# Differential attention on 128 rows for both score passes, and post-norm weights kept with the row buffers

## The chip, the cores and the metric

The kernel runs on one core of one Trainium2 chip. The core has engines that each work through a list of their own in order and wait for each other by semaphores: TensorE (PE) for matrix products, VectorE (DVE), ScalarE (ACT) and GpSimd (POOL) for work on rows and tiles, and SyncE (SP), which issues the transfers between the chip's memory and the core's buffers. PE reads its operands from SBUF and adds up in banks of PSUM; the other engines read PSUM and free the banks. The metric is the time of one execution in microseconds (us), as the device measures it; of several runs the median counts. Three runs of the kernel before took 2561.74, 2572.24 and 2570.22 us, median 2570.22 us.

## What is computed

A decoder trunk of two layers on 1024 tokens of width 1024, in float32. Each layer is a SwiGLU network (FFN), a token mixer and another FFN, each between two norms. The first layer's mixer is a hybrid: 4 heads of differential attention and 4 of gated linear attention (GLA) behind one projection; the second's is stick-breaking attention with 8 heads. The part that the change touches:

```python
def diff_attention(q, k, v, lam_params, subln_g, lambda_init):
    lp = lam_params.astype(f32)
    lam = jnp.exp(jnp.sum(lp[0] * lp[1])) - jnp.exp(jnp.sum(lp[2] * lp[3])) + lambda_init
    qf = q.astype(f32) * (DIFF_DH ** -0.5)          # 4 heads x 2 components, 64 wide each
    for i in range(s // Q_BLOCK):                   # 8 query tiles of 128
        sc = jnp.einsum('bqhd,bkhd->bhqk', qf[:, start:end], kf[:, :end])
        p = jax.nn.softmax(jnp.where(mask, sc, -jnp.inf), axis=-1)
        p = p[:, :, 0] - lam * p[:, :, 1]           # component 0 less lam times component 1
        outs.append(jnp.einsum('bhqk,bkhv->bqhv', p, vf[:, :end]))
    o = rmsnorm(jnp.concatenate(outs, axis=1), subln_g) * (1.0 - lambda_init)
```

Each sublayer ends in `h + rmsnorm(y, g)`, and the weights g of this norm (1024 numbers, read to all 128 partitions) are the tile `pg`.

## The kernel before

Activations and weights are split into a high and a low part, each as `fp32r`, and a product is taken as high x high, high x low and low x high: three matmuls (`mm3`, L210 to L212). A matmul contracts over the partitions (rows) of its operands, up to 128.

The scores of differential attention contract over 64 numbers only, so there the parts are stacked. For component c, `q_stack` puts the high parts of q in the 64 rows of that component and the low parts in the other 64 rows: `A[c]`. `k_stack` puts the high parts of k in both halves of `B[c]` (L687 on ACT, L705 on ACT), and the low parts in the component's own rows of a third tile, `L` (DVE, L688). `diff_attn` then gives `scores` two passes, `(q[c], k[c])` over 128 rows, which is high x high plus low x high, and `(q[c][r], k[2][r])` over the 64 rows r, which is high x low (both L763). For query tile i, `scores` makes one chunk of up to 512 keys (i = 0 to 3) or two chunks (i = 4 to 7), none narrower than 256 columns; the last chunk of a tile gets the causal mask added by a third, small matmul (L766). Per component and head that makes 4 x 1 + 4 x 2 = 12 chunks, so 4 x 2 x 12 = 96 chunks and 192 score matmuls. Stick-breaking uses the same `scores` with three passes that all have 128 rows.

A query tile goes on as follows. DVE takes the maxima (L874, L875), ACT the exponentials with their sums (L878), DVE the factors (L884 to L891) and `e0 - g e1` (L894); PE transposes it, four blocks to a group (`tps`, L778); DVE and ACT copy the groups to attention tiles (`att`, L780, pool `at_d` with 4 buffers); PE multiplies with v (`po`, L899); then ACT squares (L902), DVE takes the mean (L170), POOL the root (L172), DVE scales (`on`, L904), PE transposes (`pot`, L906) and ACT writes the output tile (L907). Between these steps stand the projections of the next head (`pps`, `vps`, L210 to L212), which `filled` hands out over the query tiles; in the last head it is the first part of the mixer's output projection (`dps`). The tiles of k of a head (three) are in pool `kk_d` with 6 buffers, so two heads' tiles are there at a time.

`pg` is loaded by `load_pg` (L471) to pool `ep`, which is open for the whole program. An FFN loads it before its first weights; a mixer at the head of its output projection in the program, and the scheduler moves the load up far ahead. An FFN's products with `pg` are L582, those of a mixer L419 (`fo`). The row buffers that the norms use (pools `fp` and `hrow`) are opened by `open_fo`. An FFN's down projection (`down_strassen`) loads its weights by `rawd` (L527, L535), while POOL still makes sums for the end of the up projection (L343 to L346).

At the start, `consts` builds masks: two causal ones (`mk_incl`, `mk_strict`), level masks for GLA (`lmf` on POOL, L126 to L131, cast by DVE to `lm`, L134) and loads the lambda parameters (`lp`, L138), from which ACT takes an exponential (`lexp`).

The framework's scheduler fixes each engine's list from the program's order and the buffers; the text of the program alone doesn't show it. SP's list is one queue: a load that waits holds up all behind it.

Of the kernel before, what the change touches and what calls it, by code (L numbers as in the profile page):

```python
# [9 lines left out]
F32 = mybir.dt.float32  # L10
# [9 lines left out]
P = 128  # L20
# [15 lines left out]
class Trunk:  # L36
# [25 lines left out]
    def open_fo(self):  # L62
        """row buffers of the norms"""
        self.foctx = ExitStack()
        self.fp = self.dyn(self.foctx, "fp", 4, side="right")
        self.hctx = ExitStack()
        self.hrow = self.dyn(self.hctx, "hrow", HB, side="right")

    def open_mix(self, cx, z, t, po):
        """PSUM banks of the mixers; the accumulators of the rest (self.mctx) may outlive the others"""  # L70
# [33 lines left out]
    def mixer_consts(self):  # L104
# [7 lines left out]
        # additive masks, rows q, columns k: NEG where k > q (incl) or k >= q (strict)  # L112
        self.mask = {}
        for nm, base in (("incl", 0), ("strict", -1)):
            m = c.tile([P, P], F32, name="mk_" + nm)
# [6 lines left out]
        # level masks: source row s in the even half of the block of target column t  # L122
        self.lmask = {}
        for lv in LEVELS:
            m = c.tile([P, 64], F32, name="lmf%d" % lv, tag="lmf")
# [10 lines left out]
        # lambda of the differential attention, on every partition  # L136
        lp = c.tile([P, 4, 64], F32, name="lp")
# [19 lines left out]
        # twice: the gate's first factor arrives in two parts, 16 rows each  # L157
# [85 lines left out]
    def make_raw(self, xns, gname, gi, pool):  # L243
        """gained, transposed k tiles, not split"""
# [28 lines left out]
    def gu(self, cx, wg, wu, A, xn1, gname, gi):  # L273
        """A: split k tiles of the first token half; xn1: rows of the second half.
        Returns per column tile, per token half [P, TB] = silu(gate) * up."""
# [23 lines left out]
        def combos(j):  # L299
            # S1 = A21 + A22, S3 = A11 - A21, S2 = S1 - A11, S4 = A12 - S2 (S3, then S4 in A21's place)  # L300
# [36 lines left out]
        for c in range(NF):  # L337
# [4 lines left out]
            # T1 = B12 - B11, T2 = B22 - T1, T3 = B22 - B12, T4 = B21 - T2  # L342
# [32 lines left out]
    def down_step(self, w, f0, H, f, KT, accs):  # L375
        """first column half, one K tile, all token tiles"""
# [7 lines left out]
    def down(self, w, H, pg, order=None, prep=None, mid=None, begun=None):  # L384
        """begun: accumulators of the first column half that hold all but the last K tile"""
# [45 lines left out]
    def epilogue(self, tb, fo, ss, half, hsrc, hdst, last):  # L431
        """fo: rows [P, D], or pairs of halves"""
# [36 lines left out]
    def load_pg(self, row):  # L469
        pg = self.ep.tile([P, D], F32, name="pg", tag="pg")  # L470
        self.nc.sync.dma_start(out=pg, in_=row.rearrange("(o d) -> o d", o=1).to_broadcast([P, D]))  # L471
        return pg
# [13 lines left out]
    def ffn(self, l, f, x0, xn1, hsrc, hdst, last):  # L486
# [5 lines left out]
        pg = self.load_pg(a["ffn_post_g"][l, f])  # L492
        ph = self.gu(cx, wg, wu, x0, xn1, "ffn_pre_g", 2 * l + f)
        self.open_fo()
        nxt = ("mix_pre_g", l) if f == 0 else ("ffn_pre_g", 2 * (l + 1))
# [5 lines left out]
    # ---- down projection of both token halves: one level of Strassen-Winograd over  # L501
    # (token half, half of the first 2 * KH k tiles, column half); the last k tile is added as it is ----
    def down_sums(self, ph, j):
        """S1 = A21 + A22, S3 = A11 - A21 (in A21's place) of k tile j"""
# [7 lines left out]
    def down_strassen(self, w, ph, pg, hsrc, hdst, nxt):  # L512
# [10 lines left out]
        def raw(j, k=None, cols=None):  # L523
            """[P, 2, TB]: both column halves of k tile j, or a column half of the two k tiles j, k"""
# [13 lines left out]
        # B11 = (j, 0), B12 = (j, 1), B21 = (j + KH, 0), B22 = (j + KH, 1)  # L538
# [51 lines left out]
        # P1 = A11 B11, P2 = A12 B21: C11 = P1 + P2  # L590
# [675 lines left out]
```

## Time and profile before

| | |
|---|---|
| median of 3 runs | 2570.22 us |
| lowest and highest run | 2561.74, 2572.24 us |
| profiled execution: span from the first to the last instruction | 2559.7 us |
| TensorE's mean granted clock, as a share of full speed | 0.987 |
| PE busy | 2452.2 us, 96% of the span |
| DVE, ACT, POOL busy | 67%, 42%, 26% |
| chain that ended last | PE 72%, DVE 15%, issue 4%, DMA, POOL and ACT 3% each |
| differential attention, its scores on PE | 652.6 to 892.4 us |

The profiler recorded one execution, and every duration in the working comes from that one. "Busy" is time in which an instruction of the engine ran; on PE neighbouring matmuls overlap, so that starts, and not durations, tell how fast they follow each other. The chain that ended last is found backwards from the last instruction: at each step to what released it. A wait is idle time of an engine that ended when another engine, or a transfer, let it go on.

### The profile page before, as it was taken

What the parts mean: (1) busy time and instruction counts of PE and PEld (TensorE: products, weight loads), DVE (VectorE), ACT (ScalarE), POOL (GpSimd) and SP (SyncE); (2) the same over time, 40 slices, a digit from 0 to 9 for tenths busy, and PEclk for the clock granted to TensorE, in tenths of its full rate; (3) what the DMA queues carried; (4) which work ended last, traced back from release to release, by engine and by line L of the source; (5) the groups of instructions that cost most, each with busy time, mean ns of one, the idle gap of its engine ahead of it and who ended that gap; (6) DMA issues with size and microseconds to landing.
All of it is one profiled execution on the core that took longest, in us unless ns stands there. A gap on an engine that the chain in (4) does not pass through costs nothing.

```text
span 2559.7 us, 32932 instructions
## 1 busy us (share of the span) xinstructions
PE 2452.2 (96%) x12253; PEld 1995.3 (78%) x12253; DVE 1724.8 (67%) x2635; ACT 1071.6 (42%) x2141; POOL 665.6 (26%) x542
## 2 busy tenths in 40 slices
PE   7999999999999999999999998999999999999997
PEld 6787777788777787887777887778888978878776
DVE  6767685754656758667789677845545476676777
ACT  6423454322545646323455234442323344642343
POOL 2445430110000001445424455300000000034543
PEclk9999999999999999999999999999999999999999
DMA  5221551112100254223452215521111034422145
GB/s 176 75 83 65 188 190 49 62 38 75 34 30 34 103 181 123 74 83 115 148 194 83 83 58 181 175 92 35 34 42 34 30 112 163 135 77 79 62 157 188
DMA packets 238841, 251.97 MB, mean 98 GB/s; under 512 B 9860, under 2 KB 186200, under 8 KB 238680
## 3 DMA queue, kind: packets, MB, share of 16 engines
q1 hardware_dynamic: 238680, 249.85, 30.0%
q8 instruction: 97, 1.59, 0.2%
q14 instruction: 64, 0.52, 0.1%
HBM read 215.21 MB, written 34.60 MB: 98 GB/s over the span
## 4 chain that ended last, share of the span: by engine, by line
PE 72%; DVE 15%; issue 4%; DMA 3%; POOL 3%; ACT 3%; SPq 0%; DVEq 0%; POOLq 0%; ACTq 0%
DVE hl L201 4%; PE z L763 4%; PE pps L210 4%; PE pps L212 4%; PE pps L211 4%; PE pd L210 3%; PE pd L211 3%; PE pd L212 3%; PE pc L211 3%; PE pc L212 3%; PE pc L210 3%; DMA rawd<-in_ffn_w_down_dram 2%; PE vps L210 2%; PE vps L211 2%; PE vps L212 2%
## 5 line engine op out<-in xcount | busy, mean ns | idle before, releaser
L172 POOL TENSOR_TENSOR rs<-ms,nhalf 128x1 f32<-128x1 f32 (+1 forms) x136 | 98.6, 732 | 1064.1 <-DVE ms L170 1007.5
L259 ACT CAST wq<-rawt 128x512 fp32r<-128x512 f32 x264 | 163.5, 622 | 340.0 <-PE pc L212 167.2
L260 DVE TENSOR_TENSOR wq<-rawt,wq 128x512 fp32r<-128x512 f32 x264 | 227.7, 866 | 46.6 <-ACT wq L259 41.0
L201 DVE TENSOR_TENSOR hl<-rawd,hl 128x512 fp32r<-128x512 f32 x200 | 162.5, 815 | 106.9 <-ACT hl L200 106.6
L200 ACT CAST hl<-rawd 128x512 fp32r<-128x512 f32 x200 | 123.6, 621 | 223.5 <-issue 60.4
L210 PE MATMUL pps<-hl,wh 128*128 128x512 f32 x512 | 208.3, 408 | 1.1 <-ACT hl L203 1.1
L212 PE MATMUL pps<-hl,wl 128*128 128x512 f32 x512 | 204.1, 399 | 0.0
L211 PE MATMUL pps<-hl,wh 128*128 128x512 f32 x512 | 204.0, 399 | 0.0
L343 POOL TENSOR_TENSOR rawt<-rawt 128x512 f32<-128x512 f32 x44 | 66.5, 1512 | 406.4 <-DMA rawt<-in_ffn_w_up_dram 243.2
L210 PE MATMUL pa<-hl,wq 128*128 128x512 f32 x352 | 140.9, 408 | 12.3 <-ACT ph L323 12.0
L210 PE MATMUL pd<-hl,wq 128*128 128x512 f32 x352 | 140.2, 398 | 10.7 <-DVE c L357 10.7
L210 PE MATMUL vps<-vh,hl 128*128 128x256 f32 x512 | 146.9, 287 | 0.0
L212 PE MATMUL vps<-vh,hl 128*128 128x256 f32 x512 | 145.0, 283 | 0.0
L211 PE MATMUL vps<-vl,hl 128*128 128x256 f32 x512 | 144.8, 283 | 0.0
L780 DVE COPY att<-tps 128x512 f32<-128x512 f32 (+2 forms) x96 | 56.3, 586 | 129.6 <-PE tps L778 129.0
L763 PE MATMUL z<-k,q 128*128 128x512 f32 (+5 forms) x444 | 139.9, 396 | 1.8 <-ACT b L796 1.0
L210 PE MATMUL pc<-hl,wq 128*128 128x512 f32 x352 | 137.7, 391 | 3.6 <-ACT hl L200 3.2
L212 PE MATMUL pa<-hl,wq 128*128 128x512 f32 x352 | 138.9, 397 | 1.6 <-DVE wq L260 1.6
L211 PE MATMUL pa<-hl,wq 128*128 128x512 f32 x352 | 140.2, 398 | 0.0
L211 PE MATMUL pd<-hl,wq 128*128 128x512 f32 x352 | 140.1, 398 | 0.0
L212 PE MATMUL pd<-hl,wq 128*128 128x512 f32 x352 | 139.7, 397 | 0.0
L212 PE MATMUL pc<-hl,wq 128*128 128x512 f32 x352 | 138.3, 393 | 0.0
(280 smaller groups left out, 6725.4 us busy)
## 6 DMA issues: line engine op xcount, KB each, us to landing
rawt<-in_ffn_w_gate_dram SPq DMA_DIRECT2D x88, 512.0 KB, 3.7
rawd<-in_ffn_w_down_dram SPq DMA_DIRECT2D x60, 512.0 KB, 3.6
rawd<-in_ffn_w_down_dram SPq DMA_DIRECT2D x116, 256.0 KB, 2.6
rawt<-in_ffn_w_up_dram SPq DMA_DIRECT2D x44, 512.0 KB, 3.8
hres<-h SPq DMA_DIRECT2D x40, 512.0 KB, 2.9
h<-hres SPq DMA_DIRECT2D x40, 512.0 KB, 5.0
rawt<-in_hyb_w_in_dram SPq DMA_DIRECT2D x16, 512.0 KB, 3.9
rawt<-in_sb_w_qkv_dram SPq DMA_DIRECT2D x16, 512.0 KB, 3.8
```

Of the source, the lines that this page charges most:

```text
L172: nc.gpsimd.tensor_tensor(out=rs, in0=ms, in1=self.nhalf.to_broadcast([P, n]) if n > 1 else self.nhalf, op=ALU.pow)
L200: nc.scalar.copy(out=t[:, 0], in_=src)
L201: nc.vector.tensor_tensor(out=t[:, 1], in0=src, in1=t[:, 0].bitcast(F32), op=ALU.subtract)
L210: nc.tensor.matmul(ps, lhsT=ah, rhs=bh, start=first, stop=False, skip_group_check=more)
L211: nc.tensor.matmul(ps, lhsT=ah, rhs=bl, start=False, stop=False, skip_group_check=more)
L212: nc.tensor.matmul(ps, lhsT=al, rhs=bh, start=False, stop=last, skip_group_check=more)
L259: nc.scalar.copy(out=w[:, 0], in_=src)
L260: nc.vector.tensor_tensor(out=w[:, 1], in0=src, in1=w[:, 0].bitcast(F32), op=ALU.subtract)
L343: gt(out=b11, in0=b12, in1=b11, op=ALU.subtract)
L763: nc.tensor.matmul(z[:, :wide], lhsT=lhs[:, i * P:(i + 1) * P], rhs=rhs[:, c0:c0 + wide], start=j == 0, stop=j == len(passes) - 1 and not ...
L780: (nc.scalar.copy if j0 else nc.vector.tensor_copy)(out=t[:, :n], in_=ps[:, :n])
```

## The change

`k_stack` gets two tiles for the low parts, one for each component, and puts them in both halves of the rows: a copy by ACT for each component and token half, 64x512, 16 in all. The second score pass runs over all 128 rows with these; as the lower half of `q[c]` meets the low parts too, the product of the low parts is now added. A head has four tiles of k, so `kk_d` goes from 6 to 8 buffers, and `at_d` from 4 to 3. `pg` moves to a pool `pgp` of one buffer that `open_fo` opens next to the row buffers; an FFN loads it after its gate and up projections. The masks of the start and `lp` share one buffer (tag "made").

```diff
     def open_fo(self):
         self.foctx = ExitStack()
         self.fp = self.dyn(self.foctx, "fp", 4, side="right")
+        self.pgp = self.dyn(self.foctx, "pgp", 1, side="right")
         self.hctx = ExitStack()
...
-            m = c.tile([P, P], F32, name="mk_" + nm)
+            m = c.tile([P, P], F32, name="mk_" + nm, tag="made")
...
-            m = c.tile([P, 64], F32, name="lmf%d" % lv, tag="lmf")
+            m = c.tile([P, 64], F32, name="lmf%d" % lv, tag="made")
...
-        lp = c.tile([P, 4, 64], F32, name="lp")
+        lp = c.tile([P, 4, 64], F32, name="lp", tag="made")
...
-        pg = self.ep.tile([P, D], F32, name="pg", tag="pg")
+        pg = self.pgp.tile([P, D], F32, name="pg", tag="pg")
...
-        pg = self.load_pg(a["ffn_post_g"][l, f])
         ph = self.gu(cx, wg, wu, x0, xn1, "ffn_pre_g", 2 * l + f)
         self.open_fo()
+        pg = self.load_pg(a["ffn_post_g"][l, f])
...
-                self.two_parts(B[c][r, cs], L[r, cs], ps[r], 1.0)
+                self.two_parts(B[c][r, cs], L[c][r, cs], ps[r], 1.0)
                 self.nc.scalar.copy(out=B[c][o, cs], in_=ps[r])
+                self.nc.scalar.copy(out=L[c][o, cs], in_=L[c][r, cs].bitcast(F32))
...
-                r = slice(c * 64, (c + 1) * 64)
-                zs = self.scores([(q[c], k[c]), (q[c][r], k[2][r])], i, "incl")
+                zs = self.scores([(q[c], k[c]), (q[c], k[2 + c])], i, "incl")
...
-                k[h] = [kk.tile([P, S], F32R, name="k", tag="kk") for c in range(3)]
-                return self.proj_steps(w, DK + h * P, X, self.k_stack(k[h], k[h][2]))
+                k[h] = [kk.tile([P, S], F32R, name="k", tag="kk") for c in range(4)]
+                return self.proj_steps(w, DK + h * P, X, self.k_stack(k[h][:2], k[h][2:]))
...
-                self.at = cd.enter_context(self.tc.tile_pool(name="at_d", bufs=4, reuse_waits="tile"))
-                kk = cd.enter_context(self.tc.tile_pool(name="kk_d", bufs=6, reuse_waits="tile"))
+                self.at = cd.enter_context(self.tc.tile_pool(name="at_d", bufs=3, reuse_waits="tile"))
+                kk = cd.enter_context(self.tc.tile_pool(name="kk_d", bufs=8, reuse_waits="tile"))
```

Line numbers shift by one or two after the edit (L419 becomes L420, L899 L901, L904 L906, L906 L908). The order of the instructions changes at the start, within differential attention, where the two mixers' output projections begin, and on SP at the loads of `pg`. Three places of it, each first of the kernel before and then of the changed one:

First piece, PE in the last head, from the `po` products of query tile 6 on. `dps_...` are accumulators of the output projection, `pot` is tile 6's output, the `e` that is transposed is tile 7's.

```order
L899 MATMUL po<-v,att 128x128 x7
L210 MATMUL dps_7972<-hl 128x512
L211 MATMUL dps_7972<-hl 128x512
L212 MATMUL dps_7972<-hl 128x512
L210 MATMUL dps_7972<-hl 128x512
L210 MATMUL dps_7973<-hl 128x512
L211 MATMUL dps_7973<-hl 128x512
L212 MATMUL dps_7973<-hl 128x512
L210 MATMUL dps_7974<-hl 128x512
L211 MATMUL dps_7974<-hl 128x512
L906 MATMUL pot<-ident,on 128x128
```

PE in the changed kernel, from the same products on:

```order
L901 MATMUL po<-v,att 128x128 x7
L211 MATMUL dps_8003<-hl 128x512
L212 MATMUL dps_8003<-hl 128x512
L908 MATMUL pot<-ident,on 128x128
L213 MATMUL dps_8003<-hl 128x512
L211 MATMUL dps_8003<-hl 128x512
L212 MATMUL dps_8003<-hl 128x512
L213 MATMUL dps_8003<-hl 128x512
L211 MATMUL dps_8003<-hl 128x512
L780 MATMUL tps<-ident,e_7857 128x128 x4
L212 MATMUL dps_8003<-hl 128x512
```

Ahead of `pot` there were nine products of the output projection's second column half; now there are two, and both go to an accumulator (`dps_8003`) in a bank that an accumulator of the first column half has to leave.

Second piece, DVE at the same place. The products with `pg` (L419, now L420) free the accumulators of the first column half; `s`, `rc`, `g` and `e` belong to the softmax of tile 7, `ms` and `on` to the output of tile 6.

```order
L419 TENSOR_TENSOR fo_7929<-dps_7346,pg 128x512
L875 TENSOR_REDUCE nm<-m_7840 128x1
L419 TENSOR_TENSOR fo_7930<-dps_7347,pg 128x512
L170 TENSOR_SCALAR ms<-ss 128x1
L419 TENSOR_TENSOR fo_7931<-dps_7348,pg 128x512
L904 TENSOR_SCALAR on<-po,rs,rc 128x128
L419 TENSOR_TENSOR fo_7932<-dps_7349,pg 128x512
L884 TENSOR_TENSOR s_7847<-sums 128x2
L201 TENSOR_TENSOR hl<-rawd,hl 128x512
L889 RECIPROCAL rc<-s_7847 128x2
L891 SCALAR_TENSOR_TENSOR g<-s_7847,nlam,rc 128x1
L894 SCALAR_TENSOR_TENSOR e_7829<-e_7844,g,e_7829 128x1024
```

DVE in the changed kernel, from tile 7's factors on:

```order
L886 TENSOR_TENSOR s_7875<-sums 128x2
L891 RECIPROCAL rc<-s_7875 128x2
L893 SCALAR_TENSOR_TENSOR g<-s_7875,nlam,rc 128x1
L171 TENSOR_SCALAR ms<-ss 128x1
L420 TENSOR_TENSOR fo_7960<-dps_7374,pg 128x512
L906 TENSOR_SCALAR on<-po,rs,rc 128x128
L896 SCALAR_TENSOR_TENSOR e_7857<-e_7872,g,e_7857 128x1024
L420 TENSOR_TENSOR fo_7961<-dps_7375,pg 128x512
L420 TENSOR_TENSOR fo_7962<-dps_7376,pg 128x512
L782 COPY att<-tps 128x512
L420 TENSOR_TENSOR fo_7963<-dps_7377,pg 128x512
```

The products stood ahead of tile 7's softmax factors, between its maxima; now the first stands behind them and behind the mean `ms` of tile 6, and the others behind the scaling of e.

Third piece, SP, loads of an FFN, ahead of its first weight loads before, and at the end of its up projection now (here the first FFN for the kernel before and the second for the changed one; the four FFNs are alike in this).

```order
L95 DMA graw<-in_gla_norm_g_dram 1x128
L95 DMA graw<-in_gla_b_a_dram 2x128
L471 DMA pg<-in_ffn_post_g_dram 128x1024
L270 DMA rawt<-in_ffn_w_gate_dram 128x8x128 x4
L138 DMA lp<-in_diff_lambda_dram 128x256
L270 DMA rawt<-in_ffn_w_gate_dram 128x8x128 x2
```

SP in the changed kernel, from the last gate and up weights of an FFN on:

```order
L271 DMA rawt<-in_ffn_w_gate_dram 128x8x128
L271 DMA rawt<-in_ffn_w_up_dram 128x8x128
L536 DMA rawd<-in_ffn_w_down_dram 128x512 x2
L472 DMA pg<-in_ffn_post_g_dram 128x1024
L536 DMA rawd<-in_ffn_w_down_dram 128x512 x8
L443 DMA h<-hres_3126 128x1024
```

The load of `pg` left SP's queue ahead of all weights of the FFN; now it stands behind the second load of the down projection, and all others of that projection behind it.

## Rows read from the trace of the kernel before

**Rows 1.** The page's busy times by engine, and the chain's shares by engine:

```profile
PE 2452.2 (96%) x12253; PEld 1995.3 (78%) x12253; DVE 1724.8 (67%) x2635; ACT 1071.6 (42%) x2141; POOL 665.6 (26%) x542
...
PE 72%; DVE 15%; issue 4%; DMA 3%; POOL 3%; ACT 3%; SPq 0%; DVEq 0%; POOLq 0%; ACTq 0%
```

**Rows 2.** One stretch: its length, busy us of PE, PEld, DVE, ACT, POOL, clock, DMA:

```profile
640.00:900.00 260.00, 256.25 (x1361) 191.44 (x1361) 169.53 (x403) 141.79 (x395) 18.72 (x31) 1.00 0.15 51
```

**Rows 3.** The waits of PE, 645 to 900 us: total us, times, longest:

```profile
PE pot L906 <- DVE on L904: 2.1, 6, 0.7
PE z L763 <- ACT e L878: 0.8, 1, 0.8
```

**Rows 4.** The groups of PE by form, 645 to 900 us: busy us, mean ns:

```profile
L763 PE MATMUL z<-k,q 64*128 64x512 f32 x40 | 19.9, 496 | 0.0
...
L763 PE MATMUL z<-k,q 128*128 128x512 f32 x40 | 18.5, 463 | 0.8 <-ACT e L878 0.8
```

**Rows 5.** Score matmuls of differential attention in time: start us, length us, instruction:

```profile
653.20 0.67 PE L763 MATMUL z<-k,q 128*128 128x256 f32 x2
653.81 0.23 PE L766 MATMUL z<-mkb_incl,identb 128*128 128x128 bf16 x1
...
828.57 0.47 PE L763 MATMUL z<-k,q 128*128 128x512 f32 x1
828.98 0.50 PE L763 MATMUL z<-k,q 64*128 64x512 f32 x1
829.40 0.51 PE L763 MATMUL z<-k,q 128*128 128x512 f32 x1
...
830.26 0.23 PE L766 MATMUL z<-mkb_incl,identb 128*128 128x128 bf16 x1
```

**Rows 6.** Score matmuls of stick-breaking, all of 128 rows, the same view:

```profile
1762.79 0.60 PE L763 MATMUL z<-k,q 128*128 128x256 f32 x3
1763.23 0.23 PE L766 MATMUL z<-mkb_strict,identb 128*128 128x128 bf16 x1
...
2126.30 1.39 PE L763 MATMUL z<-k,q 128*128 128x512 f32 x5
2126.61 0.39 PE L763 MATMUL z<-k,q 128*128 128x512 f32 x1
2127.53 0.23 PE L766 MATMUL z<-mkb_strict,identb 128*128 128x128 bf16 x1
```

**Rows 7.** A group of ACT by form: count, busy us, mean ns, idle before:

```profile
L705 ACT CAST k<-pps 64x512 fp32r<-64x512 f32 x16 | 9.3, 580 | 7.1 <-DVE k L688 6.9
```

**Rows 8.** The output chain of one q tile in time, first and last steps:

```profile
883.50 1.50 PE L899 MATMUL po<-v,att 128*128 128x128 f32 x12
...
886.56 0.41 DVE L904 TENSOR_SCALAR on<-po,rs,rc 128x128 f32<-128x128 f32 x1 [0.73 <-POOL rs L172]
...
887.03 0.33 PE L906 MATMUL pot<-ident,on 128*128 128x128 f32 x1
```

**Rows 9.** The loads of pg to landing; PE and DVE at the out-projection's entry:

```profile
DMA to landing us min/median/max: 4.1/4.7/5.7
...
892.76 1.73 PE L899 MATMUL po<-v,att 128*128 128x128 f32 x14
...
895.01 0.15 DVE L170 TENSOR_SCALAR ms<-ss 128x1 f32<-128x1 f32 x1 [0.44 <-ACT on L902]
...
897.94 1.28 DVE L894 SCALAR_TENSOR_TENSOR e<-e,g,e 128x1024 f32<-128x1024 f32 x1
```

**Rows 10.** POOL's last sum of an up-projection, and a load on SP, in time:

```profile
213.42 1.75 POOL L346 TENSOR_TENSOR rawt<-rawt,t 128x512 f32<-128x512 f32 x1
...
226.81 0.33 SPq L535 DMA_DIRECT2D rawd<-in_ffn_w_down_dram  x1
```

**Rows 11.** DVE at the start in time; ACT's table loads of one line:

```profile
18.31 0.68 DVE L260 TENSOR_TENSOR wq<-rawt,wq 128x512 fp32r<-128x512 f32 x1
...
L325 ACT ACT_TABLE_LOAD x3 | 3.8, 1283 | 0.1
```

## The prediction

> **What bounds the kernel now.** I read the page's head first: PE is busy for 2452.2 us, 96% of the span of 2559.7, DVE for 67%, ACT for 42%, and the chain of work that ended last is 72% PE [rows 1]. Then I took the stage that the change edits, differential attention, as one stretch: from 640 to 900 us PE is busy for 256.25 of 260 us, DVE for 169.53, ACT for 141.79, and the granted clock is 1.00, the upper of the two levels, 2.4 GHz, so that nothing here can come from a slow clock [rows 2]. The waits of PE say the same: the two longest sums in that stretch are 2.1 us in 6 places, at `pot`, the transposition of a finished output tile, and 0.8 us at a score matmul [rows 3]. So in this stage a nanosecond that PE is spared is a nanosecond of the span, as long as DVE's and ACT's chain of one q tile stays hidden.
>
> **The score passes.** Each score chunk takes two passes, one over 128 rows and one over 64: of the 192 score matmuls 96 are 64-row ones. At 512 columns there are 40 of each, and the 64-row one lasts longer, 496 against 463 ns [rows 4]. Durations overlap on PE, so the price must be read from start to start.
> *One chunk (tiles 0 to 3):* from the start of a pair at 653.20 to the mask behind it at 653.81 it takes 0.61 us [rows 5]. In stick-breaking, whose passes all have 128 rows, three matmuls of the same 256 columns take 1763.23 - 1762.79 = 0.44 us [rows 6], or 0.15 each; the first of a group is the dearest, so two take about 0.32. Saved: 0.29 us.
> *Two chunks in a row (tiles 4 to 7), 512 columns:* the starts are 828.57, 828.98 and 829.40, the fourth matmul follows, and the mask starts at 830.26: 0.41, 0.42, and 0.86 for the last two, 1.69 us in all [rows 5]. Five of stick-breaking's stand between 2126.30 and the mask at 2127.53, and the second of them starts at 2126.61: 0.31 for the first, then 0.23 each [rows 6]. Four would take 1.00. Saved: 0.69 us. So the pass alone isn't what is dear (0.42 against 0.23): the matmul ahead of it pays too.
> Each head has two components, and each of them 4 single chunks and 4 such pairs: with 4 heads, 32 of each. 32 x 0.29 = 9.3 and 32 x 0.69 = 22.1, together 31.4 us. The price hangs little on the width: 0.29 is read at 256 columns, 0.69 at 512. Where projections stand between the chunks of a pair, each half saves 0.29; were all of them torn apart so, 96 x 0.29 = 27.8. I take **-31**, since most pairs stand together, and keep -28 for the range. What the new pass adds to the sum (low parts times low parts) costs nothing: the columns are the same.
>
> **The low parts' copies.** k gets four more ACT copies for each head, 16 in all. The nearest row is the CAST of k from PSUM, as large, 580 ns [rows 7]: 16 x 0.58 = 9.3 us on ACT, which is idle for 118 of 260 us [rows 2] and ends one wait of PE of 0.8 us [rows 3]. Cover is missing only where a head's first scores wait for the last projection of k: one copy of 0.58 us on the path, in 4 heads, is the upper bound, 2.3, and 0 the lower, since an added copy can't make k ready earlier. I take **+1**.
>
> **New waits within the stage.** PE's cover shrinks by 31 us, the chain of the others doesn't. After the last `po` matmul of a q tile come ACT's square, DVE's mean, POOL's root and DVE's scaling, and then PE's `pot`. A group of `po` matmuls ends at 883.50 + 1.50 = 885.00, the scaling runs from 886.56 to 886.97, and `pot` starts at 887.03 [rows 8]: 2.0 us from the end of the one to the start of the other, and 0.06 behind its operand. I took from the new order what stands on PE between the last `po` and `pot` of each tile, at 0.23 us for 512 columns [rows 6] and less for narrower ones: in about 14 of 32 tiles it falls below this, by 0.1 to 1.6 us, some 6 us in all; 2.1 are there now [rows 3]. So **+4**. The chain from the scores to the transpositions (maximum, exponential, scaling) loses cover too; it ended one wait of 0.8 us [rows 3], and I add **+3**. For both terms together I keep 0 and 10. The attention tiles have 3 buffers in place of 4: a q tile fills two at most, and the third is free for the next tile's first: 0.
>
> **The weights of the mixer's norm.** `pg` came long before; now it comes with the row buffers, and on DVE the four products with it stand later (second piece of the order). The first stands behind the mean of tile 6, which starts at 895.01 today, the second behind the scaling of e, 1.28 us, which starts at 897.94 today [rows 9]. Each of them frees a PSUM bank, and on PE `dps_8003`, which waits for the first, stands ahead of `pot` (first piece). PE is done with tile 6's `po` at 892.76 + 1.73 = 894.49 [rows 9]; the first product can't end before 895.01 + 0.15 + 0.68 = 895.84, where 0.68 is what an operation of two 128x512 operands takes on DVE [rows 11]: a wait of 1.35 us. The bank after that costs perhaps 0.3 to 1 more. The load itself waits for a score matmul of the last tile and takes 4.1 to 5.7 us to land [rows 9]; if that matmul is done at about 888, soon after the `pot` at 887.03 [rows 8], the load is there at 892 to 894, in time; if SP issues it 5 us later, because loads ahead of it wait, PE stands for 3 to 5 us more. Bounds 1.4 and 8, I take **+3**. In stick-breaking no q tile stands behind the products: 0.
>
> **The FFNs' weights.** Four `pg` loads move from ahead of an FFN's first weight load to behind the second `rawd` load (third piece), where SP stands until POOL's last sum of the up projection is done, 213.42 + 1.75 = 215.17 in the first FFN. The load after it there, the third `rawd`, leaves at 226.81 today [rows 10], 11.6 us later, and the products with `pg` come only after the down projection. Cost 0.
>
> **The start.** The masks now share one buffer, and the loads of the first weights move up by one issue. The first split of a weight on DVE, 18.31 to 18.99, which the first product awaits [rows 11], then stands behind fewer casts: a gain of perhaps 1.5 us. Against it, ACT gets two more table loads, 3.8 / 3 = 1.28 us each [rows 11], in the first 60 us. **-1**, bounds -3 and +3.
>
> **The sum:** -31 + 1 + 4 + 3 + 3 - 1 = -21 us. Against the profiled span, 2559.7, that is 2538.7. The median of the three runs, 2570.22, lies 10.5 us above that span and the lowest run, 2561.74, 2 us; differences carry over, so I forecast 2570.2 - 21 = **2549 us**. The gain at its full size and no waits at all gives -34, 2536; the end of the forecast on the other side is 2557 (-13).
>
> **The rivals.**
> *A. Waits take the place of the passes.* A q tile's chain is latency, not work: DVE is idle for 90 of 260 us and still some of its steps come late. If PE waits 0.35 us more in each of 32 tiles than I allowed, 11 us go, and the time is 2560; with 0.55, 18 us, it is 2567. For it: `pot` starts 0.06 us behind its operand already [rows 8]. Against it: over the whole stage PE waits for about 3 us [rows 3].
> *B. The pass isn't dear for its 64 rows.* The steps of 0.42 could belong to this stage (two passes that share the query tile, interleaved with other work). Then only the costs are left, +1, +3 and -1: 2570 + 3 = 2573. Against it: at the same width stick-breaking's steps are 0.23, among the same neighbours, transpositions, masks and projections [rows 5, 6]. By the Trainium skill, "TensorE: Matmul & The Clock Gate" (Why this matters for your kernels), a single matmul with a small K takes the same time as one with K=128; by that rule the 64-row pass is no dearer, and the time would be this rival's. The rows disagree with it here, 0.42 against 0.23 at 512 columns, and fit another of its pages, "TensorEngine Tiling (Array Packing)" (Key Properties): a change of the tiling mode drains the engine.
> *C. Slower.* SP's queue is in order, so all `rawd` loads of a down projection but two now stand behind `pg`. If `pg` leaves X us later than the third `rawd` does today, the weights come X later in four FFNs, and DMA has 3% of the chain that ended last [rows 1]. The forecast turns into a measurable loss at 4X = 21 + 13 = 34, X = 8.5: POOL's sum would have to end 20 us later than now (11.6 + 8.5). At X = 10 the time is 2549 + 40 = 2589. Nothing in POOL's order there changes, so little speaks for it.
>
> **The chances.** Half a per cent of the time, 12.9 us, is about what a measurement of this kernel can tell from no change: the border is 2557.4. The forecast, 2536 to 2557, has 0.75, and 0.02 goes to more than that. A has 0.13, between 2557 and 2567. B has 0.06 and C 0.04. Faster: the forecast and what is better, 0.77. Same: A and nearly all of B, 0.18. Slower: C and the rest of B, 0.05. The range, 2537 to 2563, leaves out C, B and the far end of A.
>
> **What would show each step.** Right: all 192 score matmuls are 128-row ones, four of them at 512 columns in a row take about 1.0 us from start to start, the stage from its first score to its last is about 24 us shorter, and PE's waits in it rise from some 3 to some 10 us, most at `pot`. Wrong: steps of 0.4 that stay (B), waits over 20 us in the stage (A), a third `rawd` that leaves later than today (C), or several us of waiting at `dps` or `pot` where the out-projection begins.

## The result and the profile after

The changed kernel takes 2542.72 us (median of 4 runs, 2540.78 to 2544.75), beside 2570.07 us of the kernel before: a ratio of 0.9908 with a 95% interval of 0.9892 to 0.9924, so it is faster, by 0.9%. In the sets beside the experiments the kernel before took 2565.32 us (35 runs, 2560.09 to 2570.76), 2567.21 us (18 runs, 2558.78 to 2570.52) and 2565.01 us (7 runs), and the changed one 2542.96 us beside the last of these, ratio 0.9909 (0.9890 to 0.9928). The difference is thus 22 to 27 us, and 22.1 where both ran again side by side. The forecast was 21. The profiled execution has a span of 2543.0 us, against 2559.7 before; that pair alone gives 16.7, since the one of before lies near the short end of what that kernel takes.

The page of the changed kernel, busy times by engine and the chain that ended last, as [rows 1]:

```profile
PE 2428.8 (96%) x12253; PEld 1993.4 (78%) x12253; DVE 1738.2 (68%) x2635; ACT 1081.6 (43%) x2159; POOL 666.4 (26%) x542
...
PE 67%; DVE 16%; DMA 5%; issue 4%; POOL 4%; ACT 4%; SPq 0%; POOLq 0%; DVEq 0%; ACTq 0%
```

PE has lost 23.4 us of busy time. DVE's 13.4 more say nothing, since a second trace of the kernel before has 1736.5 us too. The balance of the engines is as it was. Differential attention, the same stretch as [rows 2] (length, then PE, PEld, DVE, ACT, POOL, clock, DMA):

```profile
640.00:900.00 260.00, 248.95 (x1438) 201.75 (x1437) 176.78 (x422) 156.65 (x429) 20.85 (x35) 0.99 0.20 69
```

The stretch now holds 1438 matmuls in place of 1361, since attention is over earlier in it. Its score matmuls by form (count, busy us, mean ns) answer to [rows 4]:

```profile
L765 PE MATMUL z<-k,q 128*128 128x512 f32 x80 | 28.2, 443 | 1.9 <-ACT e L880 1.9
...
L765 PE MATMUL z<-k,q 128*128 128x384 f32 x48 | 13.6, 363 | 0.0
L765 PE MATMUL z<-k,q 128*128 128x256 f32 x64 | 13.4, 305 | 0.1
```

All 192 have 128 rows. Four of them at 512 columns in a row, as [rows 5], start us first:

```profile
684.99 1.17 PE L765 MATMUL z<-k,q 128*128 128x512 f32 x4
686.01 0.23 PE L768 MATMUL z<-mkb_incl,identb 128*128 128x128 bf16 x1
```

They take 686.01 - 684.99 = 1.02 us to the mask, where four took 1.69, and a forecast from stick-breaking's [rows 6] said 1.00. What PE waits for from 640 to 900 us (total us, times, longest), as [rows 3]:

```profile
PE pot L908 <- DVE on L906: 3.6, 12, 0.5
PE z L765 <- ACT e L880: 1.9, 1, 1.9
PE dps L211 <- DVE fo L420: 1.7, 1, 1.7
PE po L901 <- ACT ot L909: 1.6, 2, 1.1
PE tps L780 <- DVE att L782: 1.1, 2, 0.9
```

The waits at `pot` and at a score matmul are longer than in [rows 3], the one at `tps` is 1.1 us where it was 0.5, and two are new: `po`, which waits for ACT, and `dps`, at the out-projection's entry. The score matmuls of the stage, first of the kernel before and then of the changed one (duration ns min/median/max, first and last start us, commonest forms):

```profile
L763 PE MATMUL z<-k,q x192: 274/436/505, 652.6 to 891.9; 128*128 128x512 f32 x40, 64*128 64x512 f32 x40, 128*128 128x256 f32 x32, 64*128 64x256 f32 x32
```

```profile
L765 PE MATMUL z<-k,q x192: 275/375/797, 648.0 to 867.4; 128*128 128x512 f32 x80, 128*128 128x256 f32 x64, 128*128 128x384 f32 x48
```

From the start of the first to the start of the last the stage takes 219.4 us in place of 239.3, with 1252 PE instructions in both kernels.

### The profile page after: what moved, and what is told of

The parts are those of the page before. It is cut to its first block, busy times and chain, and to the rows that moved or that the text cites. A ratio compares the mean times of both kernels' runs of the same rounds, so it can differ in the third digit from the quotient of the medians.

```text
span 2543.0 us, 32954 instructions
## 1 busy us (share of the span) xinstructions
PE 2428.8 (96%) x12253; PEld 1993.4 (78%) x12253; DVE 1738.2 (68%) x2635; ACT 1081.6 (43%) x2159; POOL 666.4 (26%) x542
## 4 chain that ended last, share of the span: by engine, by line
PE 67%; DVE 16%; DMA 5%; issue 4%; POOL 4%; ACT 4%; SPq 0%; POOLq 0%; DVEq 0%; ACTq 0%
DVE hl L202 4%; PE pps L211 3%; PE pps L212 3%; PE pps L213 3%; PE pd L211 3%; PE pd L212 3%; PE pd L213 3%; PE pc L212 3%; PE pc L213 3%; DMA rawd<-in_ffn_w_down_dram 3%; PE pc L211 3%; PE po L808 2%; PE z L765 2%; PE vps L211 2%; PE vps L213 2%
## 5 line engine op out<-in xcount | busy, mean ns | idle before, releaser
L261 DVE TENSOR_TENSOR wq<-rawt,wq 128x512 fp32r<-128x512 f32 x264 | 241.4, 918 | 46.1 <-ACT wq L260 40.5
L211 PE MATMUL pc<-hl,wq 128*128 128x512 f32 x352 | 137.9, 392 | 3.6 <-ACT hl L201 3.2
L213 PE MATMUL pc<-hl,wq 128*128 128x512 f32 x352 | 138.5, 394 | 0.0
L212 PE MATMUL pc<-hl,wq 128*128 128x512 f32 x352 | 138.5, 393 | 0.0
```

Source lines behind the costliest of these rows:

```text
L211: nc.tensor.matmul(ps, lhsT=ah, rhs=bh, start=first, stop=False, skip_group_check=more)
L212: nc.tensor.matmul(ps, lhsT=ah, rhs=bl, start=False, stop=False, skip_group_check=more)
L213: nc.tensor.matmul(ps, lhsT=al, rhs=bh, start=False, stop=last, skip_group_check=more)
L261: nc.vector.tensor_tensor(out=w[:, 1], in0=src, in1=w[:, 0].bitcast(F32), op=ALU.subtract)
```

## The experiments

**The kernel before again.** No edit, 12 runs.

> The kernel before, unchanged, once more, for its own spread: three of its four timed runs took about 2570 us and one 2562, and the profiled one was of the faster kind. If the 8 to 10 us have a place, a second trace that is that much longer shows it in one stretch (theory: the waits of an FFN's down projection for its weights by DMA and POOL); if they are spread out (rival: the whole span a little longer everywhere, 0.4% of each stage), each stage is longer by its share. If this trace is of the faster kind too, nothing follows.

2566.17 us (2557.58 to 2570.12), ratio to before 1.0001 (0.9991 to 1.0011). Its trace has a span of 2560.9 us, close to the first one's 2559.7, and the stage of attention at 239.3 us again. So the kernel's own spread is some 12 us from run to run, and a difference of one pair of traces of under that says little. The clock goes with it: the mean granted clock was 0.988 in the shortest of the 12 runs and 0.984 in the longest, and 0.004 of 2560 us is some 10 us (an estimate). So most of the spread is time at the lower of the two clock levels, 1.2 GHz; in which stages it lies was not seen.

**The second pass on 64 rows again, all else as changed.**

```diff
-                zs = self.scores([(q[c], k[c]), (q[c], k[2 + c])], i, "incl")
+                r = slice(c * 64, (c + 1) * 64)
+                zs = self.scores([(q[c], k[c]), (q[c][r], k[2 + c][r])], i, "incl")
```

> The changed kernel with one thing undone: the second score pass takes only the component's 64 rows again; copies, buffers and pg stay as changed. Theory (alternating 64 and 128 rows is what costs): the stage from the first to the last score of differential attention goes from 219.4 back to about 239 us, pairs at 512 columns from 1.0 to 1.7 us, the time by +20 to about 2563. Rival B (the steps belong to the stage, not to the rows): the stage stays within 2 us of 219.4 and the time at 2543.

2568.37 us, ratio to before 1.0005 (0.9995 to 1.0015): the whole gain is gone, 25.7 us against the changed kernel where about 20 was expected. The stage takes 241.0 us, and four matmuls at 512 columns, 128 and 64 rows by turns, take 692.18 - 690.49 = 1.69 us again (start us first; the view names a merged row by its first form):

```profile
690.49 1.76 PE L765 MATMUL z<-k,q 128*128 128x512 f32 x4
692.18 0.23 PE L768 MATMUL z<-mkb_incl,identb 128*128 128x128 bf16 x1
```

Rival B is out: the same stage with the same buffers and copies is 21.6 us longer with 64 rows in the second pass. The copies, the buffers and the new order, as it stands here, together then cost 241.0 - 239.3 = 1.7 us in the stage.

**Both passes on 64 rows, in the kernel before.**

```diff
-                zs = self.scores([(q[c], k[c]), (q[c][r], k[2][r])], i, "incl")
+                zs = self.scores([(q[c][r], k[c][r]), (q[c][r], k[2][r])], i, "incl")
```

> The kernel before with the first score pass cut to the component's 64 rows too (it leaves out the product of q's low with k's high parts), so that all 192 score matmuls have 64 rows. Theory D (changing between 128 and 64 rows costs, at each change): within a group there is no change left, four matmuls at 512 columns take about 1.0 plus one change in and one out, 1.3 us in place of 1.69, a single pair stays at 0.6; the stage from the first to the last score falls from 239.3 to some 226 to 232 us, the time by 7 to 13. Theory L (a 64-row matmul itself takes 0.42): no step falls, the stage is 239 or longer, up to 249. Rival B (steps belong to the stage): 239 within 2.

2561.01 us, ratio 0.9979 (0.9968 to 0.9990), the stage 234.7 us. Four 64-row matmuls in a row:

```profile
695.79 1.21 PE L763 MATMUL z<-k,q 64*128 64x512 f32 x4
696.93 0.23 PE L766 MATMUL z<-mkb_incl,identb 128*128 128x128 bf16 x1
```

They take 696.93 - 695.79 = 1.14 us to the mask. Read from start to start, the steps from one 64-row matmul to the next have a median of 234 ns (20 of them), as quick as 231 from one 128-row score matmul to the next in the changed kernel (23). So theory L is out: a 64-row matmul is not slow. What is slow is the change: the last one of a group, with other work of 128 rows behind it, takes 324, and the mask ahead of a first one takes 159 ns to the next start in place of 39. The stage falls by 4.6 us only, less than the 7 to 13 forecast for this run. The order fits that: single chunks now pay for a change both on the way in and out, and the traces hold 184 changes between 64 and 128 rows in place of 192.

**Both chunks' 128-row passes first, then both 64-row ones, in the kernel before.** `scores` gets a flag that makes the outer loop run over the passes:

```diff
+            for j, (lhs, rhs) in enumerate(passes):
+                for c0, w, z in res:
+                    wide = max(w, 256)
+                    nc.tensor.matmul(z[:, :wide], lhsT=lhs[:, i * P:(i + 1) * P], rhs=rhs[:, c0:c0 + wide],
+                                     start=j == 0, stop=j == len(passes) - 1 and c0 + w != n)
```

> The kernel before with the score matmuls of a q tile of two chunks in another order: both 128-row passes, then both 64-row passes, nothing else changed. Half the changes between row counts are gone where the four stand together, which is so for some 20 of the 32 pairs. Theory D: each saves 0.40 us, the stage falls from 239.3 to about 231, less new waits of up to 2 us. Theory L and rival B: the stage stays at 239 within 2.

2563.20 us, ratio 0.9987 (0.9975 to 0.9999); the stage takes 233.2 us, 6.1 less, with PE idle for 0.9 us more in it than before. Four matmuls in this order:

```profile
771.31 1.37 PE L775 MATMUL z<-k,q 128*128 128x512 f32 x4
772.61 0.23 PE L778 MATMUL z<-mkb_incl,identb 128*128 128x128 bf16 x1
```

772.61 - 771.31 = 1.30 us, 0.39 less than by turns, where the forecast said 0.40. The stage fell by 6 rather than 8 because more groups stand apart in the scheduler's order than I had counted: 13 with two passes of each kind together, not some 20. There are 152 changes in place of 192. The order of the same matmuls alone moves the stage, as theory D has it; the whole kernel's time is some 3 us lower by the ratio, and the interval only just leaves out no change at all.

**The masks and the lambda parameters in one buffer, in the kernel before.**

```diff
-            m = c.tile([P, P], F32, name="mk_" + nm)
+            m = c.tile([P, P], F32, name="mk_" + nm, tag="made")
...
-        lp = c.tile([P, 4, 64], F32, name="lp")
+        lp = c.tile([P, 4, 64], F32, name="lp", tag="made")
```

> The kernel before with one part of the change alone: masks and lambda parameters in one shared buffer. In the changed trace the start runs ahead by 4.5 us at 81 us and by 5 us at 250 us. Theory M (the masks' new order lets the first weight splits come earlier): most of this is here, 3 to 5 us by 250 us, time 2565. Rival P (it is the transfer of pg, no longer ahead of the first weights): under 1 us here.

2560.43 us, ratio 0.9978 (0.9968 to 0.9989): about 5 us. The first product `da` of the down projection starts at 244.4 us in place of 250.0, so all of it is there by then: theory M. But not where I had put it. The first product `pa` still starts at 18.1 us (18.4 before). By 60 us PE is 1.2 us ahead, at 73 us no more, and at 88 us it is 5.9. In the kernel before, POOL makes its first weight sums there beside DVE (a timeline of the kernel before: start us, us):

```profile
66.71 0.68 DVE L311 TENSOR_TENSOR s<-s,hl 128x512 f32<-128x512 f32 x1
...
70.22 1.74 POOL L345 TENSOR_TENSOR rawt<-rawt 128x512 f32<-128x512 f32 x1
...
70.72 1.78 DVE L201 TENSOR_TENSOR hl<-s,hl 128x512 fp32r<-128x512 f32 x1
...
71.92 1.74 POOL L346 TENSOR_TENSOR rawt<-rawt,t 128x512 f32<-128x512 f32 x1
...
72.42 1.78 DVE L314 TENSOR_TENSOR xr<-xr,hl 128x512 f32<-128x512 f32 x1
...
74.05 0.39 PE L210 MATMUL pa<-hl,wq 128*128 128x512 f32 x1
...
78.40 0.73 PE L210 MATMUL pa<-hl,wq 128*128 128x512 f32 x1 [3.96 <-ACT ph L323]
...
78.93 0.63 PE L211 MATMUL pa<-hl,wq 128*128 128x512 f32 x1
...
79.36 0.63 PE L212 MATMUL pa<-hl,wq 128*128 128x512 f32 x1
```

DVE's sums of two operands take 0.68 us alone and 1.78 beside a POOL sum. The four of them make ACT's `ph` late, PE stops for 3.96 us, and the steps behind that are 0.43 us in place of 0.23: the clock fell to its lower level, 1.2 GHz, after the stop. With the masks in one buffer DVE is 0.9 us further on there (its `s` of L311 starts at 65.84 in place of 66.71), while POOL's first sum starts only 0.4 earlier (66.50 in place of 66.93). Now it is POOL that waits (its sum of 1.3 to 1.7 us took 9.01), while DVE's stay at 0.69. The timeline of POOL in this kernel, and then DVE's groups by form in the same stretch (count, busy us, mean ns):

```profile
66.50 9.01 POOL L343 TENSOR_TENSOR rawt<-rawt 128x512 f32<-128x512 f32 x1 [29.58 <-DMA rawt<-in_ffn_w_up_dram]
75.59 1.29 POOL L344 TENSOR_TENSOR t<-rawt 128x512 f32<-128x512 f32 x1
```

```profile
L260 DVE TENSOR_TENSOR wq<-rawt,wq 128x512 fp32r<-128x512 f32 x3 | 2.1, 691 | 0.0
...
L313 DVE TENSOR_TENSOR xr<-hl,s 128x512 f32<-128x512 f32 x1 | 0.7, 690 | 0.0
L314 DVE TENSOR_TENSOR xr<-xr,hl 128x512 f32<-128x512 f32 x1 | 0.7, 690 | 0.0
```

PE's stop shrinks from 3.96 to 0.7 us, and the granted clock of 60 to 96 us is 1.00, against 0.95 (length, PE, PEld, DVE, ACT, POOL, clock, DMA; the kernel before, then this one):

```profile
60.00:96.00 36.00, 32.04 (x133) 25.40 (x132) 31.95 (x42) 20.08 (x37) 12.65 (x8) 0.95 0.28 82
```

```profile
60.00:96.00 36.00, 35.08 (x151) 27.69 (x151) 32.80 (x45) 21.20 (x39) 20.41 (x9) 1.00 0.26 74
```

**pg next to the row buffers, in the kernel before.** The five lines of the diff on `pgp`, `load_pg` and its call.

> The kernel before with another part alone: pg in the pool next to the row buffers, loaded late. Theory M: the start gains under 1 us; rival P: 3 to 5 us by 250 us. Both: where the out-projection of the hybrid mixer begins, PE waits 1.5 to 5 us for the product with pg that stands later on DVE, about +2.5 us net between the last score and 905 us; score passes unchanged; in the FFNs no third rawd load leaves later. Time within 5 us of before.

2568.36 us, ratio 1.0013 (1.0005 to 1.0022). The first product starts at 15.0 us, 3.4 earlier than before, as SP's queue has one load less ahead of the weights; by 25 us all but 0.3 of this is lost again, and `da` starts at 250.1 as in the kernel before: rival P is out. From the last score to the end of the out-projection it takes 79.3 us in place of 75.7, 3.6 more. The place in time (start us, us):

```profile
891.72 1.73 PE L900 MATMUL po<-v,att 128*128 128x128 f32 x14
...
894.72 0.69 DVE L420 TENSOR_TENSOR fo<-dps,pg 128x512 f32<-128x512 f32 x1 [0.43 <-DMA pg<-in_mix_post_g_dram]
...
895.46 0.65 PE L211 MATMUL dps<-hl 128*128 128x512 f32 x1 [2.02 <-DVE fo L420]
```

DVE waits 0.43 us for the load itself here, and PE 2.02 for DVE.

**The changed kernel without the copies.**

```diff
-                self.nc.scalar.copy(out=L[c][o, cs], in_=L[c][r, cs].bitcast(F32))
...
-                zs = self.scores([(q[c], k[c]), (q[c], k[2 + c])], i, "incl")
+                zs = self.scores([(q[c], k[c]), (q[c], k[c])], i, "incl")
```

> The changed kernel without the 16 copies of the low parts: the second pass takes k's high parts again (it leaves out k's low parts in the scores and counts the high ones twice). What the copies cost shows against 2542.7 us and a stage of 219.4 us. Theory (hidden on ACT): 0 to 2.4 us, the stage at 217 to 219.4. Rival (ACT's 9.9 us lie on the path of each head's first scores or of the exponentials): the stage at 210 to 213, the time by 6 to 9 us lower.

This kernel leaves the low parts of k out of the scores. 2540.71 us, the stage 215.9 us. Beside 219.4 and 217.2 (the two traces of the changed kernel) that is 1.3 to 3.5 us for the copies, 2 us by the medians. They are nearly hidden; the rival is out.

**The first group of POOL's sums on DVE, in the changed kernel.** What the masks' run showed suggests that the masks are not needed for it: the first weight sums of an FFN's up projection, which POOL makes while DVE prepares the last of the gate, can be made by DVE itself.

```diff
+            gt = tt if c == 0 else nc.gpsimd.tensor_tensor
             gt(out=b11, in0=b12, in1=b11, op=ALU.subtract)
```

> The changed kernel with the first of POOL's 11 groups of weight sums in each FFN's up projection on DVE instead. The start gained 5.6 us by the masks alone, where a PE wait of 4.0 us at 78 us shrank to 0.7 and the clock stayed at the upper level. Theory S (DVE's sums take 1.75 in place of 0.68 us while POOL runs its own, so DVE is late for the last products pa of the gate): with POOL idle there, PE's waits at pa for ACT's ph fall from 9.9 to under 4 us over the four FFNs, the clock stays up behind them, and the time falls by 4 to 9 us to about 2536. Rival R (DVE is simply full there): four more sums of 0.68 us on DVE make these waits longer, the time rises by 3 to 10 us.

2527.66 us (2522.81 to 2529.03), ratio to the kernel before 0.9844 (0.9827 to 0.9861): 15 us better than the changed kernel, and the version that beats both. PE's waits for ACT's `ph`, in the changed kernel and here:

```profile
PE pa L211 <- ACT ph L324: 9.9, 4, 3.7
```

```profile
PE pa L211 <- ACT ph L324: 0.8, 1, 0.8
```

Two stretches at the FFNs' gates (length, PE, PEld, DVE, ACT, POOL, clock), first in the changed kernel, then here:

```profile
60.00:100.00 40.00, 37.94 (x159) 30.18 (x158) 36.60 (x47) 20.90 (x38) 18.42 (x12) 0.96 0.25 71
2180.00:2290.00 110.00, 106.30 (x466) 85.41 (x465) 83.31 (x121) 57.82 (x104) 32.49 (x26) 0.97 0.33 96
```

```profile
60.00:100.00 40.00, 40.00 (x175) 32.29 (x174) 37.75 (x54) 22.86 (x41) 13.67 (x8) 1.00 0.32 89
2180.00:2290.00 110.00, 109.98 (x494) 88.86 (x493) 84.19 (x121) 53.74 (x94) 32.09 (x23) 1.00 0.29 84
```

PE is busy all the time in both, and the clock is 1.00 where it was 0.96 and 0.97. Theory S holds, rival R is out. The gain is over the 4 to 9 us forecast: the waits alone fell by 9.1 us, and the stops had cost the clock as well, as the two stretches show.

**The same in the kernel before.** The same line.

> The kernel before with the one edit that took the changed kernel from 2542.7 to 2527.7 us: the first of POOL's 11 groups of weight sums of each FFN's up projection on DVE. If that gain is the FFNs' own (theory S: POOL's sums hold up DVE's in the four FFNs, whatever attention does), before gains about as much, 12 to 18 us, and the start alone 5 us, as with the masks. If it needs the masks' or pg's new places (rival), it gains under 6 us.

2542.41 us, ratio 0.9914 (0.9895 to 0.9933): 22.6 us, over the 12 to 18 expected and as much as the whole change gives. PE's waits for `ph`, 12.0 us in the kernel before, are gone, and `da` starts at 244.0 us in place of 250.0. The mean granted clock of the runs is 0.989 to 0.991 beside 0.984 to 0.987; some 0.005 of 2560 us, 13 us, is about half of the gain (an estimate). It needs nothing of the change; and where the masks have already taken 4 to 5 us of it at the start, as in the changed kernel, 15 are left.

**All of POOL's sums of the up projection on DVE, in the changed kernel.** `gt = tt` for every c.

> The changed kernel with all 44 groups of these sums on DVE, 176 operations of 0.68 us in place of POOL's, 30 us more on DVE in each FFN. Theory S says that a POOL sum beside it makes an operation of DVE 1.1 us longer, so DVE's load should hardly grow: time 2520 to 2535. Rival (DVE becomes the bound of the up projection, where its sums come just ahead of the products): time 2545 to 2590.

2528.98 us, ratio 0.9855 (0.9838 to 0.9872). The page's busy times:

```profile
PE 2427.6 (96%) x12253; PEld 1990.4 (79%) x12253; DVE 1772.0 (70%) x2811; ACT 1082.3 (43%) x2159; POOL 393.8 (16%) x366
```

DVE's busy time rose from 1738.2 to 1772.0 us, by 34, although 176 sums of 0.68 us, 120 us, came to it. The other 86 us must come off its own instructions. Of its 128x512 operations on two operands 216 took over 1 us in the changed kernel and 143 do here, although there are 176 more of them: theory S again, for most of it. For the time it is no better than moving the first group alone.

**The changed kernel again.** No edit.

> The changed kernel once more, unchanged, beside the kernel before on this chip, to give the difference from more runs: on the first chip it was 27 us by the medians of four runs each (-0.92%), but the kernel before took 2565 and 2567 us in larger sets. Theory: 2542 to 2545, about -23 us. A second trace: stage of differential attention 219.4 within 1, start to 250 us within 2 us of the first trace.

2542.96 us beside 2565.01, ratio 0.9909 (0.9890 to 0.9928). The stage takes 217.2 us, 2.2 less than in the first trace and so a little outside what I had expected; `da` starts at 246.0.

## The prediction, step by step

*What bounds the kernel:* right. PE bounded the stage, and what PE was spared the span was spared.

*The score passes, -31:* the mechanism and the price of one place were right, the sum was too large. From the first score to the last there are 1252 PE instructions in both kernels, so without PE's idle time the stage can be compared: 239.3 - 3.8 = 235.5 before, 219.4 - 8.7 = 210.7 after, and 217.2 - 7.6 = 209.6 in the second trace. That is -25 to -26, outside even the bound of -28. All of it lies on the score matmuls: from each to the next start they take 67.0 us before, and 41.9 and 41.4 after, idle time left out, and the other work of the stage keeps its 168 to 169 us. The step that failed is the count: 32 pairs of chunks, "most pairs stand together". In the order of before, 15 groups of four stand together, 39 pairs of 128 and 64 rows stand alone, and 13 64-row matmuls stand alone behind other work; 6 groups more are 64, 128, 64 rows and 2 are 128, 64, 128. The 13 I hadn't thought of; such a one takes 430 ns before, and a lone 128-row one 322 after, at 512 columns, a saving of 0.11, not 0.29. With 0.29 for a pair and 0.68 for four, as forecast, and 0.50 and 0.2 for the two kinds of three, as traced, the count gives 26 us. The order was there to be counted, tile by tile, before the forecast.

*Rival B and the page's rule:* the rule of the Trainium skill, "TensorE: Matmul & The Clock Gate" (Why this matters for your kernels), that a single small-K matmul (it names K=32) takes as long as one with K=128, is right here for 64 rows (234 against 231 ns) and yet was no guide, since it is told of one matmul. That a change of the mode drains the engine, as its "TensorEngine Tiling (Array Packing)" has it (Key Properties), is what the runs agree with, and they give the price: in 128, 128, 64, 64 the second takes 322 in place of 231 and the third 335 in place of 234 (medians at 512 columns), so one change between two score matmuls costs some 0.19 us, half of it on the matmul ahead of it and half on the one behind. Over the stage it is less: in the kernel before each of the 96 64-row matmuls stands between 128-row ones, which makes 192 changes, and 25 us is 0.13 for each.

*The copies, +1 (0 to 2.3):* 1.3 to 3.5 us by the stage without them. Of the right size, the upper bound too low.

*New waits, +7 (0 to 10):* PE's idle time in the stage rose by 3.8 to 4.9 us, copies' waits included. `pot` was to get +4 and got 1.7 (2.1 to 3.6 + 0.2); the wait at a score matmul rose by 1.1, and `po` got 1.8, which I had not named. The size was over-estimated, the place partly right. The granted clock of 640 to 900 us is 0.99, where it was 1.00: it fell to the lower level about the 1.9 us wait for a score matmul near the end of the stage, which the forecast had left out.

*The weights of the mixer's norm, +3 (1.4 to 8):* right. From the last score to the end of the out-projection it is 78.1 us, and 78.9 in the second trace, in place of 75.7: +2.4 and +3.2, and +3.6 with pg alone. The changed kernel there, in time:

```profile
868.93 1.73 PE L901 MATMUL po<-v,att 128*128 128x128 f32 x14
...
870.99 0.16 DVE L886 TENSOR_TENSOR s<-sums 128x2 f32<-128x2 f32 x1 [1.72 <-ACT e L880]
...
871.59 0.68 DVE L420 TENSOR_TENSOR fo<-dps,pg 128x512 f32<-128x512 f32 x1
...
872.32 0.50 PE L211 MATMUL dps<-hl 128*128 128x512 f32 x1 [1.67 <-DVE fo L420]
...
872.73 1.28 DVE L896 SCALAR_TENSOR_TENSOR e<-e,g,e 128x1024 f32<-128x1024 f32 x1
...
873.92 0.69 DVE L420 TENSOR_TENSOR fo<-dps,pg 128x512 f32<-128x512 f32 x1
```

The product (L420) stands on DVE behind the softmax factors, which waited for ACT until 870.99, and PE, done with `po` at 868.93 + 1.73 = 870.66, waits 1.67 us at `dps` for it; 1.35 was forecast from [rows 9]. The load itself, issued at 865.43, was in time.

*The FFNs' weights, 0:* right. In the last FFN the third `rawd` leaves at 2391.30 after 2411.70, 20.4 earlier, as all work around it.

*The start, -1 (-3 to +3):* wrong in its place and its size. It is -4 to -5 (250.0 to 245.0 and 246.0), by the masks alone -5.6. The step that failed is the mechanism: I looked at the first weight split at 18.31 us and took a shift of the start for what it is there. Most of that shift is not kept; what counted was how POOL's sums meet DVE's 50 us later. The wait of 3.96 us for `ph` stood in the trace before and I had passed it by.

*The sum:* the stage -20 to -22 (-23 forecast), its tail +2.4 to +3.2 (+3), the start -4 to -5 (-1): some -23 in each of the two traces, with -21 forecast. Three errors stood against each other: 5 to 6 us too much for the passes, 3 to 4 too much cost for the copies and the new waits (8 forecast), and 3 to 4 too little for the start. That the sum came so near is in part luck. The forecast of 2549 was missed by 6 us, of which 3 to 5 are the base: the three runs shown had a median of 2570.2, and larger sets have 2565 to 2567.

*Rivals A and C:* A's waits came to some 4 us rather than 18 more; C's loads were on time.

## What to carry to other kernels

Where matmuls of 64 and 128 rows alternate on one core of this chip, count the changes between them, in the order that the engine really runs: one between two score matmuls cost 0.19 us here, and the 192 of the stage 25 us. Filling the idle rows, even with a product nobody needs, bought some 20 us of this stage for 16 copies. And look at a PE wait of some microseconds together with the clock behind it and with what POOL does at that time: one line that took POOL's sums out of DVE's way was worth as much as the whole change.

## What was not expected of the hardware

A DVE operation on two 128x512 operands took 0.68 us alone and 1.71 to 1.78 beside a POOL operation on two such operands, and a POOL one took 9.01 us where DVE's instructions followed each other without a gap; it ended 1.15 us behind the last of them, at 75.51 and 74.36 us. So one of the two waits for the other, and which one it is depends on who comes first: nearly the same two lists of instructions, shifted against each other by half a microsecond (DVE 0.9 us earlier, POOL 0.4), gave a PE stop of 3.96 us or of 0.7. The Trainium skill says so in "SBUF — State Buffer" (SBUF: two separate sides): the two engines share a pair of ports, which goes to whoever starts first, for the whole instruction. All of POOL's operands in this kernel lie in SBUF; of the engines beside PE only DVE and ACT read PSUM in it. The traces agree with the page; that POOL can be kept out over a dozen DVE instructions is what they add.

After PE's stop of 3.96 us the granted clock of the stretch fell (0.95 in 60 to 96 us, steps of 0.43 in place of 0.23 us), so that such a stop costs more than its length: with the masks in one buffer the waiting was 3.3 us shorter there, and PE's lead grew by 4.7 us, from 1.2 to 5.9.

What stays open: in which stages the 12 us lie by which runs of the kernel before differ from each other. Both its traces have spans near the short end, so no kept trace shows a long run.
